# Masks of a chunked recurrence moved from GpSimd to VectorE, and an unread product left out

## The chip, the core and the metric

The kernel runs on one core of one Trainium2 chip. The core has a matrix engine (TensorE, in the profile PE, with its weight loads shown apart as PEld), a vector engine (VectorE, DVE), an engine for activation functions and copies (ScalarE, ACT), a general engine (GpSimd, POOL) and a queue that issues transfers (SyncE, SP). All work from SBUF, the memory on the chip; TensorE writes its results to PSUM, from which VectorE and ScalarE read them. The metric is the device time of one execution in microseconds (us), given as a median of several runs.

## The reference

The kernel computes one step of a decoder layer for 1024 prompt tokens and 32 sample tokens (8 sequences of 4). Cut to what matters here:

```
z = rmsnorm(x) @ w_in                        # columns for the recurrence and for pooling
h = x + [rwkv7(z_r) | pool(z_p)] @ w_out
h = h + peer(rmsnorm(h))                     # product keys: top-16 of 16384 experts, 8 heads
h = h + (p @ ple_w) * sigmoid(rmsnorm(h) @ ple_gate_w)
y = rmsnorm(h)

# inside rwkv7, per head, S is a 64 x 64 state:
s_kk = S @ (-kk_t)
S    = S * w_t + outer(s_kk, kk_t * a_t) + outer(v_t, k_t)
out  = S @ r_t
# then: out normalised per head (mean, variance), scaled, plus a bonus term, times a gate
```

## The kernel before

The work is a list of stages that overlap. **Stage A** (`phase_a`) projects all 1056 tokens, prepares the recurrence's inputs and writes them to the DRAM tile `fd`, seven groups of four blocks: a, r, b, k, v, g and o (the gate and bonus terms). It is followed by the pooling heads. **The recurrence** (`bchunk`, lines 446 to 619) runs over 16 chunks of 64 prompt tokens and one chunk for the 32 sample tokens. **Stage C** (`phase_c`) takes groups of 256 or 288 tokens through `w_out`, the norm and the query projection, and stores key scores in `sc_d`. **Top-k** (`top`, `select`) finds the experts of each token on VectorE and, for the first 672 token positions, builds one-hot products (lines 901 to 910) that give a dense gate table `g_d`. **The dense experts** (`ublock`, `vblock`, all through `emm`, line 1112) multiply these 672 tokens with all 16384 experts on TensorE, while the other 384 tokens gather their experts' rows (lines 1221 to 1238). `Tail` ends the layer.

The recurrence does not start with the others and end with them: `merge` (line 955) interleaves what the generators issue. Chunks 0 and 1 run beside pooling, the sample chunk with chunks 2 and 3, then chunk 4 beside the embedding products and the pooled half of `w_out`, and the rest beside stage C and top-k of three token groups. At most three chunks are in flight (`NSLOT`), begun at least six steps apart (`STAG`). Each has its own SBUF tiles, told apart by its slot; all take their PSUM tiles from one pool of four buffers. The final order on each engine's queue is not the order of the source: the program is built with a scheduler that plans every engine's queue ahead from estimated durations (line 1403). On the chip each queue then runs strictly in that order.

One chunk works on quads: the 8 heads are 4 pairs, and a pair's two 64 x 64 blocks lie on partitions 0 to 63 and 64 to 127, so a 64 x 64 product for all heads is 8 products, each of two instructions in the profile. All go through the helper `hmm`, so the profile names line 470 for each; GpSimd's steps go through `PTT` and have line 127. The steps of one chunk:

- **Products and their mask.** For each pair, b and k as weights against [a, r] together (line 491) give four 64 x 64 products: b by a, b by r, k by a, k by r. VectorE multiplies two pairs at a time out of PSUM with a causal mask into `lp` (line 492). The later steps read `lp[:, :, 1]`, `[2]` and `[3]` (lines 550, 569, 574); `lp[:, :, 0]`, b by a, is read by none.
- **Masked levels.** a against b (line 496) goes by ScalarE into SBUF as `lts` (line 498). The inverse of a triangular matrix is built in six levels (`NL`): level l needs `lts` times a constant mask `nmt[:, l]`, which GpSimd makes for each level (lines 501 and 512) in a tile `ltm` of two buffers. X starts as the first masked level plus the identity (GpSimd, line 508), Y as its transpose (TensorE, line 507, and ScalarE, line 509).
- **Levels 1 to 5.** TensorE multiplies `ltm` with Y, ScalarE copies the result to `zp`, TensorE multiplies it with X, and ScalarE copies X and Y back (lines 513 to 525).
- **State.** Transposes of b, k and v (lines 528 to 538), then w, u and the new state S (lines 548 to 597). Only this part needs the state of the chunk before.
- **Output.** Sums per head on VectorE (lines 602 to 604), the centred output `cen` (line 606, in the tile named `lts`), its square on ScalarE, the inverse root, then `cen` times the root on GpSimd (line 613), a transpose on TensorE, times g on VectorE (line 617) and plus o on GpSimd (line 618), then the store to `y_d`, which stage C reads.

Of the kernel before, what the change touches and what calls it, by code (L numbers as in the profile page):

```python
# [15 lines left out]
AF = mybir.ActivationFunctionType  # L16
ALU = mybir.AluOpType
# [46 lines left out]
def body(ctx, tc, io):  # L64
    nc = tc.nc
    mm = nc.tensor.matmul
    TT, STT, TS, ACT = (nc.vector.tensor_tensor, nc.vector.scalar_tensor_tensor, nc.vector.tensor_scalar,
                        nc.scalar.activation)
# [57 lines left out]
    def PTT(out, a, b, op):  # L126
        nc.gpsimd.tensor_tensor(out, a, b, op=op)  # L127

    def PS(tag):
        return pools[tag].tile([128, 512], F32, name="ps", tag="bc" if tag in ("b0", "b1") else tag)  # L130
# [9 lines left out]
    NL = 6  # L140
    HS = (slice(0, 64), slice(64, 128))
    nmt = rconst.tile([128, NL, 64], F32)
    mask64 = rconst.tile([128, 4, 64], F32)
    mask4 = rconst.tile([128, 4, 64], F32)
    ident2 = rconst.tile([128, 64], F32)
# [300 lines left out]
    def bchunk(c, sp=None):  # L446
        smpl = sp is not None
        slot = 1 if smpl else c % NSLOT
        pst = "b0"
# [3 lines left out]
        nlev = 2 if smpl else NL  # L453
        msk = mask4 if smpl else mask64

        def wt(name, n, bufs=1):
            return pb.tile([128, n], F32, name=name, tag=f"{name}{slot}", bufs=bufs)

        def q4(name, bufs=1):
            return v3(wt(name, 256, bufs), 64)  # L460

        def quad(ps):
            return v3(ps[:, :256], 64)

        def bc(ap):
            return ap[:, None, :].to_broadcast([128, 4, 64])

        def hmm(o, l, r, start, stop):
            for hs in HS:
                mm(o[hs], l[hs], r[hs], start=start, stop=stop)  # L470

        def pmm(o, l, r, start, stop):
            for p in range(4):
                hmm(o[:, p], l[:, p], r[:, p], start and (start != "one" or p == 0), stop and (stop != "one" or p == 3))
# [5 lines left out]
        f = sp[3] if smpl else pb.tile([128, 28, 64], F32, name="fdc", bufs=NSLOT + 1)  # L480
        nc.sync.dma_start(f[:, :, :tt], fd[:, :, ts])
        fa, fr, fb, fk, fv, fg, fo = (f[:, 4 * i:4 * i + 4] for i in range(7))
        lp = wt("lp", 1024).rearrange("m (q j t) -> m q j t", q=4, j=4)

        for pp in range(2):
            ps = PS(pst)
            pv = ps.rearrange("m (i q t) -> m i q t", i=2, q=4)
            for i in range(2):
                p = 2 * pp + i
                for k in range(2):  # L490
                    hmm(pv[:, i, 2 * k:2 * k + 2, :], f[:, 8 + 4 * k + p], f[:, p:8:4], True, True)
            TT(lp[:, 2 * pp:2 * pp + 2], pv, msk[:, None, :, :].to_broadcast([128, 2, 4, 64]), op=ALU.mult)
            yield

        ps = PS(pst)
        pmm(quad(ps), fa, fb, True, True)
        lts = q4("lts")
        ACT(lts, quad(ps), AF.Copy)
        yield
        x0 = q4("ltm", 2)  # L500
        PTT(x0, lts, bc(nmt[:, 0, :]), op=ALU.mult)
        yx = wt("yx", 512).rearrange("m (j q t) -> m j q t", j=2, q=4)
        Y, X = yx[:, 0], yx[:, 1]
        ps = PS(pst)
        hmm(ps[:, :256], id16[:, 0, :], id16.rearrange("m q t -> m (q t)"), True, False)
        for p in range(4):
            hmm(quad(ps)[:, p], x0[:, p], ident2, False, p == 3)
        PTT(X, x0, bc(ident2), op=ALU.add)
        ACT(Y, quad(ps), AF.Copy)
        for l in range(1, nlev):  # L510
            ltm = q4("ltm", 2)
            PTT(ltm, lts, bc(nmt[:, l, :]), op=ALU.mult)
            ps = PS(pst)
            hmm(ps[:, :256], id16[:, 0, :], id16.rearrange("m q t -> m (q t)"), True, False)
            pmm(quad(ps), ltm, Y, False, "one")
            zp = q4("zp")
            ACT(zp, quad(ps), AF.Copy)
            yield
            ps = PS(pst)
            n = 1 if l == nlev - 1 else 2  # L520
            pyx = ps.rearrange("m (j q t) -> m j q t", j=2, q=4)
            pmm(pyx[:, 0], X, zp, True, True)
            if n == 2:
                pmm(pyx[:, 1], zp, X, True, True)
            ACT(yx[:, :n], pyx[:, :n], AF.Copy)
            yield

        kbT = wt("kbT", 512).rearrange("m (j q t) -> m j q t", j=2, q=4)
        ps = PS(pst)
# [5 lines left out]
        ps = PS(pst)  # L535
        turn(quad(ps), fv)
        vt = q4("vt")
# [9 lines left out]
        s_in = S[-1]  # L547
        psw = PS(pst)
        pw = quad(psw)
        pmm(pw, lp[:, :, 2], vt, "one", False)  # L550
        if smpl:
            ssm, bmask, cmask = sp[:3]
            sp_ = ssm[0]
# [8 lines left out]
        u = q4("zp")  # L562
# [3 lines left out]
        def out():  # L566
            pso = PS(pst)
            po = quad(pso)
            pmm(po, lp[:, :, 3], vt, "one", False)
            if smpl:  # L570
                sample_s(fr, po, False)
            else:
                pmm(po, fr, s_in, False, False)
            pmm(po, lp[:, :, 1], u, False, "one")
            return po

        if smpl:
# [24 lines left out]
        s1 = wt("s1", 4)  # L602
        nc.vector.tensor_reduce(s1, po, axis=AX.X, op=ALU.add)
        TS(s1, s1, -1.0 / HD, None, op0=ALU.mult)
        cen = q4("lts")
        TT(cen, po, s1[:, :, None].to_broadcast([128, 4, 64]), op=ALU.add)
        sq = q4("wn")
        ACT(sq, cen, AF.Square)
# [1 line left out]
        nc.vector.tensor_reduce(s2, sq, axis=AX.X, op=ALU.add)  # L610
        inv_sqrt(s2, s2, 1.0 / HD, leps_t)
        yield
        PTT(cen, cen, s2[:, :, None].to_broadcast([128, 4, 64]), op=ALU.mult)
        ps = PS(pst)
        turn(quad(ps), cen)
        yo = v3(pb.tile([128, 256], F32, name="yo", tag=f"kbT{slot}"), 64)
        TT(yo, quad(ps), fg, op=ALU.mult)
        PTT(yo, yo, fo, op=ALU.add)
        nc.sync.dma_start(y_d[:, :, pos:pos + tt], yo[:, :, :tt])

    wraws = {}
# [799 lines left out]
```

## Time and profile before

| | us |
|---|---|
| median of 3 runs (3301.97 to 3302.18) | 3302.07 |
| the profiled execution | 3310.19 |
| its span, first to last instruction | 3308.5 |
| recurrence, first to last instruction of line 470 (about) | 285 to 1111 |
| dense experts without a pause, from (about) | 1345 |

The profile is one execution. "Busy" is the time in which an engine has an instruction under way; matmuls overlap, and a busy PE is not PE at its peak. "Idle before" is the time that an engine stood still in front of an instruction, with the one that released it. The chain is followed back from the last instruction, at each step to what released it. An instruction group reads: line, engine, operation, output and inputs, shape, count, then busy time and mean ns of one.

### The profile page before, as it was taken

Reading aid. Unit: us, or ns where it says so; the run is one execution under the profiler, and the core shown is the slowest. Engines: PE = TensorE matmul, PEld = TensorE weight load, DVE = VectorE, ACT = ScalarE, POOL = GpSimd, SP = SyncE. Lnnn points to the kernel's source line nnn. Section 1 sums busy time; section 2 is a strip of 40 time slices with the busy share of each in tenths; the row PEclk is TensorE's granted clock in tenths of the full one; section 3 lists DMA queues with packets and bytes.
Section 4 is the critical chain, followed back from the end, with each engine's and each line's share of the span. In section 5 each row is a group of like instructions: output and inputs, shape, how many; then the busy total and the mean of one; then the engine's idle time right before and its main releaser. Section 6 shows DMA issues by size and latency. Waiting matters only on the chain.

```text
span 3308.5 us, 66279 instructions
## 1 busy us (share of the span) xinstructions
PE 3115.4 (94%) x26777; PEld 2995.7 (91%) x26777; DVE 2561.4 (77%) x4989; ACT 1127.6 (34%) x1734; POOL 1509.4 (46%) x1223
## 2 busy tenths in 40 slices
PE   8998898987888798999999999999999999999997
PEld 7886787877877787999999999999999999999996
DVE  7775333469689688888888888888888888888966
ACT  6442423434554555332222122122222222212243
POOL 5212232222132041146666665666566666666534
PEclk9999999998998898999999999999999999999998
DMA  3325557866875977569999999999999999999834
GB/s 117 117 88 126 156 139 231 277 177 179 241 218 179 296 237 229 198 225 343 336 345 337 327 348 331 327 344 344 330 334 347 331 329 341 337 327 343 316 109 129
DMA packets 437332, 858.88 MB, mean 260 GB/s; under 512 B 108960, under 2 KB 232096, under 8 KB 432544
## 3 DMA queue, kind: packets, MB, share of 16 engines
q1 hardware_dynamic: 326432, 451.93, 42.1%
q0 software_dynamic: 110592, 402.70, 33.6%
q8 instruction: 210, 3.44, 0.4%
q14 instruction: 98, 0.80, 0.1%
HBM read 733.92 MB, written 120.60 MB: 258 GB/s over the span
## 4 chain that ended last, share of the span: by engine, by line
PE 77%; DVE 9%; DMA 8%; ACT 2%; issue 2%; POOL 1%; SPq 1%; ACTq 0%; DVEq 0%; POOLq 0%
PE pd L1112 58%; PE ps L470 5%; PE ps L219 4%; PE ps L653 2%; PE ps L655 2%; PE ps L654 2%; DMA whi<-wc_d 2%; PE ps L909 2%; PE ps L302 1%; DMA scq<-sc_d 1%; DMA sc_d<-scs 1%; DMA wlo<-wc_d 1%; DMA hT_d<-h 1%; PE ps L739 1%; DVE I L762 1%
## 5 line engine op out<-in xcount | busy, mean ns | idle before, releaser
L1221 POOL DMA_INDIRECT row<-u,idx x384 | 546.6, 1423 | 313.8 <-DVE row L1229 134.1
L1221 POOL DMA_INDIRECT row<-v,idx x384 | 536.5, 1397 | 310.8 <-DVE po L1238 142.0
L1088 ACT ACTIVATE ehi<-eraw 128x1024 fp32r<-128x1024 f32 x278 | 294.7, 1060 | 1115.0 <-PE pd L1112 1014.7
L1112 PE MATMUL pd<-XH,elo 128*128 128x336 f32 x2176 | 514.7, 318 | 4.7 <-DVE elo L1090 3.1
L1112 PE MATMUL pd<-XL,ehi 128*128 128x336 f32 x2176 | 515.4, 318 | 0.0
L1112 PE MATMUL pd<-XH,ehi 128*128 128x336 f32 x2176 | 513.4, 317 | 0.3 <-ACT ehi L1088 0.2
L1112 PE MATMUL pd<-wh,ehi 128*128 128x336 f32 (+1 forms) x2112 | 503.4, 317 | 6.5 <-DVE tg L1302 6.5
L1112 PE MATMUL pd<-wh,elo 128*128 128x336 f32 (+1 forms) x2112 | 503.7, 317 | 0.0
L1112 PE MATMUL pd<-wl,ehi 128*128 128x336 f32 (+1 forms) x2112 | 502.3, 317 | 0.0
L1238 DVE SCALAR_TENSOR_TENSOR po<-row,act,po 128x1024 f32<-128x1024 f32 x381 | 488.6, 1283 | 6.7
L1229 DVE SCALAR_TENSOR_TENSOR row<-row,xt 128x1024 f32<-128x1024 f32 x384 | 455.7, 1220 | 9.7 <-DMA row<-u,idx 6.3
L1112 PEld LDWEIGHTS pd<-XH,elo 128*128 128x128 f32 x2176 | 374.1, 189 | 5.7 <-DVE elo L1090 3.5
L1090 DVE TENSOR_TENSOR elo<-eraw,ehi 128x1024 fp32r<-128x1024 f32 x256 | 315.8, 1234 | 79.0 <-ACT ehi L1088 73.2
L1112 PEld LDWEIGHTS pd<-XH,ehi 128*128 128x128 f32 x2176 | 373.3, 189 | 1.1 <-ACT ehi L1088 0.7
L1112 PEld LDWEIGHTS pd<-XL,ehi 128*128 128x128 f32 x2176 | 372.0, 189 | 0.2
L1112 PEld LDWEIGHTS pd<-wh,ehi 128*128 128x128 f32 x2112 | 362.3, 188 | 7.2 <-issue 7.0
L1112 PEld LDWEIGHTS pd<-wl,ehi 128*128 128x128 f32 x2112 | 362.4, 188 | 0.0
L1112 PEld LDWEIGHTS pd<-wh,elo 128*128 128x128 f32 x2112 | 361.7, 188 | 0.2
L653 PE MATMUL ps<-hi,whi 128*128 128x256 f32 (+1 forms) x592 | 189.3, 322 | 48.7 <-DMA whi<-wc_d 21.1
L127 POOL TENSOR_TENSOR ltm<-lts,nmt 128x256 f32<-128x256 f32 x98 | 82.1, 846 | 311.8 <-PE ps L470 189.0
L1181 DVE TENSOR_TENSOR OT<-pd,OT 128x672 f32<-128x672 f32 x120 | 102.9, 858 | 142.8 <-PE pd L1112 142.1
L910 ACT ACTIVATE gst<-ps 128x512 f32<-128x512 f32 x168 | 169.5, 1110 | 67.1 <-PE ps L909 62.0
(426 smaller groups left out, 5256.2 us busy)
## 6 DMA issues: line engine op xcount, KB each, us to landing
eraw<-uT SPq DMA_DIRECT2D x128, 512.0 KB, 6.4
eraw<-vP SPq DMA_DIRECT2D x128, 512.0 KB, 6.4
g_d<-gst SPq DMA_DIRECT2D x21, 2048.0 KB, 9.8
gq<-g_d SPq DMA_DIRECT2D x32, 1344.0 KB, 9.6
whi<-wc_d SPq DMA_DIRECT2D x108, 256.0 KB, 4.9
wlo<-wc_d SPq DMA_DIRECT2D x108, 256.0 KB, 5.2
fdc<-fd SPq DMA_DIRECT2D x16, 896.0 KB, 7.6
wc_d<-whi SPq DMA_DIRECT2D x40, 256.0 KB, 4.6
```

What stands on the lines that cost most here:

```text
L127: nc.gpsimd.tensor_tensor(out, a, b, op=op)
L219: mm(ps[:, :XW], s[:, k, :], x[:, k, a:b], start=first, stop=last)
L470: mm(o[hs], l[hs], r[hs], start=start, stop=stop)
L653: mm(ps[:, :n], whi[:, kk, :], xhi[:, k, :n], start=k == 0, stop=False)
L910: ACT(st[:, :, t2 + q:t2 + q + 4].rearrange("p e t -> p t e"), v3(ps, 128), AF.Copy, scale=1.0 / GS)
L1088: ACT(hi, raw, AF.Copy)
L1090: sub(lo, raw, hi.bitcast(F32), op=ALU.subtract)
L1112: mm(ps[:, a, :n], w_[:, k, :], x_[:, s:s + n], start=first, stop=last)
L1181: TT(halves(OT[db]), ps[:, :, :NH], halves(OT[db]), op=ALU.add)
L1221: nc.gpsimd.indirect_dma_start(out=r[:m], out_offset=None, in_=io[tab], in_offset=bass.IndirectOffsetOnAxis(ap=idx[:m, hh, k:k + 1], axis=0))
L1229: STT(r[:m], r[:m], 1.0, xt[:m], op0=ALU.mult, op1=ALU.mult, accum_out=pre[:m, k:k + 1])
L1238: STT(po[:m], r[:m], act[:m, k:k + 1], po[:m], op0=ALU.mult, op1=ALU.add)
```

## The change

Four edits in `bchunk`, and nothing outside it:

- The a-by-b product comes first in a chunk and stays in PSUM. Two VectorE instructions multiply it, broadcast, with the masks of three levels each (one level each in the sample chunk, which has two) into an `ltm` tile of six levels. ScalarE's copy to `lts` and the six GpSimd masks go.
- X's first sum, the scaling of `cen` and the last addition of `yo` move from GpSimd to VectorE.
- b by a is no longer computed: b multiplies r alone, k multiplies [a, r], and `lp` has three parts instead of four, with the mask's last three quarters.
- `cen` lies in the tile named `zp`, since `lts` is gone. In SBUF, a slot has 1536 elements of `ltm` in place of 512, 768 of `lp` in place of 1024, and 256 fewer for `lts`.

```diff
-        lp = wt("lp", 1024).rearrange("m (q j t) -> m q j t", q=4, j=4)
+        lp = wt("lp", 768).rearrange("m (q j t) -> m q j t", q=4, j=3)
+        ps = PS(pst)
+        pmm(quad(ps), fa, fb, True, True)
+        ltm = wt("ltm", 256 * NL).rearrange("m (l q t) -> m l q t", l=NL, q=4)
+        for l0, l1 in ((0, nlev // 2), (nlev // 2, nlev)):
+            sh = [128, l1 - l0, 4, 64]
+            TT(ltm[:, l0:l1], quad(ps)[:, None].to_broadcast(sh), nmt[:, l0:l1, None, :].to_broadcast(sh), op=ALU.mult)
+        yield
         for pp in range(2):
             ps = PS(pst)
-            pv = ps.rearrange("m (i q t) -> m i q t", i=2, q=4)
+            pv = ps[:, :384].rearrange("m (i q t) -> m i q t", i=2, q=3)
             for i in range(2):
                 p = 2 * pp + i
-                for k in range(2):
-                    hmm(pv[:, i, 2 * k:2 * k + 2, :], f[:, 8 + 4 * k + p], f[:, p:8:4], True, True)
-            TT(lp[:, 2 * pp:2 * pp + 2], pv, msk[:, None, :, :].to_broadcast([128, 2, 4, 64]), op=ALU.mult)
-            yield
-
-        ps = PS(pst)
-        pmm(quad(ps), fa, fb, True, True)
-        lts = q4("lts")
-        ACT(lts, quad(ps), AF.Copy)
-        yield
-        x0 = q4("ltm", 2)
-        PTT(x0, lts, bc(nmt[:, 0, :]), op=ALU.mult)
+                hmm(pv[:, i, 0, :], f[:, 8 + p], f[:, 4 + p], True, True)
+                hmm(pv[:, i, 1:3, :], f[:, 12 + p], f[:, p:8:4], True, True)
+            TT(lp[:, 2 * pp:2 * pp + 2], pv, msk[:, None, 1:, :].to_broadcast([128, 2, 3, 64]), op=ALU.mult)
+            yield
+
+        x0 = ltm[:, 0]
...
-        PTT(X, x0, bc(ident2), op=ALU.add)
+        TT(X, x0, bc(ident2), op=ALU.add)
         ACT(Y, quad(ps), AF.Copy)
         for l in range(1, nlev):
-            ltm = q4("ltm", 2)
-            PTT(ltm, lts, bc(nmt[:, l, :]), op=ALU.mult)
             ps = PS(pst)
...
-            pmm(quad(ps), ltm, Y, False, "one")
+            pmm(quad(ps), ltm[:, l], Y, False, "one")
...
-        cen = q4("lts")
+        cen = q4("zp")
...
-        PTT(cen, cen, s2[:, :, None].to_broadcast([128, 4, 64]), op=ALU.mult)
+        TT(cen, cen, s2[:, :, None].to_broadcast([128, 4, 64]), op=ALU.mult)
...
-        PTT(yo, yo, fo, op=ALU.add)
+        TT(yo, yo, fo, op=ALU.add)
```

More of the change, by code (lines that the diff above doesn't have):

```diff
@@ L549, in bchunk @@
         pw = quad(psw)
-        pmm(pw, lp[:, :, 2], vt, "one", False)
+        pmm(pw, lp[:, :, 1], vt, "one", False)
         if smpl:
@@ L568, in out @@
             po = quad(pso)
-            pmm(po, lp[:, :, 3], vt, "one", False)
+            pmm(po, lp[:, :, 2], vt, "one", False)
             if smpl:
@@ L573, in out @@
                 pmm(po, fr, s_in, False, False)
-            pmm(po, lp[:, :, 1], u, False, "one")
+            pmm(po, lp[:, :, 0], u, False, "one")
             return po
```

## The prediction

> **What bounds the kernel now.** First the page: the span, the busy times, DVE's busy tenths over 40 slices of 82.7 us, and the chain that ended last, by engine and by line.
>
> ```profile
> span 3308.5 us, 66279 instructions
> PE 3115.4 (94%) x26777; PEld 2995.7 (91%) x26777; DVE 2561.4 (77%) x4989; ACT 1127.6 (34%) x1734; POOL 1509.4 (46%) x1223
> DVE  7775333469689688888888888888888888888966
> PE 77%; DVE 9%; DMA 8%; ACT 2%; issue 2%; POOL 1%; SPq 1%; ACTq 0%; DVEq 0%; POOLq 0%
> ```
>
> POOL is 46% busy but only 1% of the chain: most work that leaves POOL leaves no gap. Then the table of stretches: PE, PEld, DVE, ACT and POOL busy, with instruction counts, granted clock, DMA share and GB/s.
>
> ```profile
> 430.00:520.00 90.00, 90.00 (x1438) 80.25 (x1438) 30.56 (x60) 20.49 (x45) 23.69 (x30) 1.00 0.49 133
> 700.00:800.00 100.00, 73.44 (x1052) 65.39 (x1050) 95.83 (x511) 35.95 (x77) 33.18 (x51) 0.78 0.50 145
> 800.00:1110.00 310.00, 277.12 (x4030) 248.23 (x4030) 250.00 (x877) 163.45 (x285) 62.80 (x84) 0.92 0.75 220
> 1345.00:3308.00 1963.00, 1938.67 (x12549) 1934.18 (x12548) 1677.88 (x2381) 520.42 (x639) 1163.82 (x826) 0.99 0.85 307
> ```
>
> After 1345 us PE is busy 98.8% with the dense experts. The change does not touch that stage; it can only start it earlier or later. So everything is decided before 1345 us, and the recurrence runs only from about 285 to 1110 us. In there the limit changes: from 430 to 520 us PE has no gap at all; from 700 to 800 us DVE has none (95.83 of 100 us, top-k and one-hot work) and PE idles for it; from 800 to 1110 us both are filled, PE to 89% and DVE to 81%.
>
> **What leaves.** The groups of the recurrence between 285 and 1161 us (busy, mean ns, idle before):
>
> ```profile
> L127 POOL TENSOR_TENSOR ltm<-lts,nmt 128x256 f32<-128x256 f32 x98 | 82.1, 846 | 311.8 <-PE ps L470 189.0 <-ACT lts L498 122.3
> L127 POOL TENSOR_TENSOR yx<-ltm,ident 128x256 f32<-128x256 f32 x17 | 14.5, 851 | 0.0
> L127 POOL TENSOR_TENSOR lts<-lts,s 128x256 f32<-128x256 f32 x17 | 11.8, 695 | 107.9 <-DVE s L179 107.9
> L127 POOL TENSOR_TENSOR yo<-yo,fdc 128x256 f32<-128x256 f32 x16 | 13.2, 824 | 55.7 <-DVE yo L617 55.7
> L498 ACT ACTIVATE lts<-ps 128x256 f32<-128x256 f32 x17 | 6.5, 385 | 8.5 <-PE ps L470 8.1
> ```
>
> POOL loses 82.1 + 14.5 + 11.8 + 13.2 = 121.6 us and ACT 6.5 us. The large idle times before the POOL groups (311.8 us) are not a cost: POOL waits there for PE to give back a buffer or for ACT. What costs is PE waiting for somebody. The waits of PE from 285 to 1345 us (us in total, times, longest):
>
> ```profile
> PE ps L909 <- DVE ab L902: 19.6, 5, 8.9
> PE ps L470 <- POOL ltm L127: 5.2, 2, 4.4
> PE ps L470 <- ACT yx L509: 3.4, 2, 2.9
> PE ps L470 <- DVE lp L492: 3.0, 2, 2.4
> PE ps L470 <- POOL lo L127: 2.7, 1, 2.7
> ```
>
> *Masks on POOL.* PE waited 5.2 us for a masked level. I take all of it away: **-5.2 us** (bounds -5.2 and 0, if DVE is as late instead). *POOL's own queue.* POOL also splits activations for the projections (lo); one such split was late by 2.7 us, and the masks no longer stand ahead of it. Half: **-1.4 us** (0 to -2.7). *ACT's copy.* Y (L509) was late by 3.4 us. Its chain was copy 0.385 + POOL mask 0.846 and two hand-overs; it becomes one DVE mask of 0.96 us (below), 0.27 us and one hand-over shorter: **-1.0 us** (0 to -3.4).
>
> *Unread products.* The product of b with a (lp[:, :, 0]) is computed as one half of a 128-wide product with b as weights, and nobody reads it. PE's products in order of time (start, us, what) show the spacing:
>
> ```profile
> 568.10 0.63 PE L470 MATMUL ps<-yx,zp 64*64 64x64 f32 x16
> 568.57 1.04 PE L470 MATMUL ps<-fdc 64*64 64x128 f32 x16
> 569.44 0.63 PE L470 MATMUL ps<-wn,yx 64*64 64x64 f32 x16
> ...
> L470 PE MATMUL ps<-fdc 64*64 64x128 f32 x512 | 37.1, 278 | 0.0
> ```
>
> From one start to the next, sixteen 64-wide products take 0.47 us (29 ns each), sixteen 128-wide ones 0.87 us (54 ns). 512 over 16 chunks are 32 a chunk, of which 16 become 64 wide: 16 x 25 ns = 0.40 us a chunk, 6.4 us in all. PE is the limit in part of the recurrence only; half: **-3.2 us** (0 to -6.4).
>
> **What arrives on DVE.** Nearest rows: the lp mask itself, two 256-wide steps, and a 672-wide step that reads PSUM like the new masks (it lies in the dense stage).
>
> ```profile
> L492 DVE TENSOR_TENSOR lp<-ps,mask 128x512 f32<-128x512 f32 x34 | 23.3, 687 | 42.6 <-PE ps L470 42.6
> L606 DVE TENSOR_TENSOR lts<-ps,s 128x256 f32<-128x256 f32 x17 | 7.1, 421 | 0.6
> L596 DVE TENSOR_TENSOR S<-S,pcs 128x256 f32<-128x256 f32 x16 | 7.3, 458 | 0.2
> L1181 DVE TENSOR_TENSOR OT<-pd,OT 128x672 f32<-128x672 f32 x120 | 102.9, 858 | 142.8 <-PE pd L1112 142.1
> ```
>
> From 421 ns at 256 to 858 ns at 672 is 1.05 ns an element. A mask step of three levels has 768: 858 + 96 x 1.05 = 0.96 us, two of them 1.92 us. The sum X, the scaling of cen and the last addition of yo have two SBUF inputs, as L596 has: 0.46 us each. The two lp masks shrink from 512 to 384, by 0.13 us each. A chunk therefore adds 1.92 + 0.46 - 0.26 = 2.12 us at its start and 0.92 us at its end. Sixteen chunks are 48.6 us; the sample chunk (two levels, so two 256-wide masks) adds 2.0: DVE 2561 to 2612 us. Which of it is felt depends on when it falls due; the lp masks (two a chunk) and L606 (one) count starts and ends:
>
> ```profile
> 700.00:800.00 100.00, 2.01 (x3) 0.78 0.50 145
> 800.00:1110.00 310.00, 5.46 (x8) 0.92 0.75 220
> ...
> 700.00:800.00 100.00, 0.82 (x2) 0.78 0.50 145
> 800.00:1110.00 310.00, 2.51 (x6) 0.92 0.75 220
> ```
>
> From 700 to 800 us: 1.5 x 2.12 + 2 x 0.92 = 5.0 us, where DVE has no room: taken in full. From 800 to 1110 us: 4 x 2.12 + 6 x 0.92 = 14.0 us, where DVE shares the limit with PE and with loads of weights: a third, 4.7 us. The other 31.6 us fall before 700 us, where DVE is a third busy (30.56 of 90 us) and PE or loads cover it: nothing; without that cover it would be all 31.6. Together **+9.7 us** (bounds 0 and 19.0, or 50.6 with no cover anywhere).
>
> *The new wait.* The first mask now makes DVE, not ACT, wait for PE's a-by-b product; behind it stand the lp masks, the top-k steps and the one-hot products that PE's L909 reads. ACT idled 8.1 us for it in all. DVE already waits 42.6 us in front of the lp masks for the products issued next to it, so that wait moves ahead rather than comes on top: nothing (0 to +8.1). X follows on DVE, cen follows its own reciprocal, yo its own product: no wait. No DMA is added; y's store is released 0.36 us earlier a chunk. The PSUM buffer of the product is held 1.9 us instead of 0.4; four such buffers serve three chunks, and I put no price on it beyond rival 1.
>
> *Stretched DVE steps.* Two rows over all their instances (min/median/max):
>
> ```profile
> L902 DVE TENSOR_TENSOR ab<-ab,e x84: 662/684/2887, 765.4 to 1313.8; 128x1024 f16<-128x1024 f16 x84
> L127 POOL TENSOR_TENSOR ltm<-lts,nmt x98: 717/731/2577, 288.1 to 1044.5; 128x256 f32<-128x256 f32 x98
> L902 DVE TENSOR_TENSOR ab<-ab,e 128x1024 f16<-128x1024 f16 x62 | 45.4, 740 | 0.5
> 285.00:1161.00 876.00, 209.77 (x272) 0.91 0.68 202
> ```
>
> Steps of equal shape reach four times their median. For L902 the excess is 62 x (740 - 684) ns = 3.5 us; POOL gives up 121.6 of its 209.8 busy us there, so 0.58 x 3.5: **-2.0 us** (0 to -3.5). [...]
>
> **Sum.** -5.2 - 1.4 - 1.0 - 3.2 + 9.7 - 2.0 = -3.1 us. The profiled execution took 3310.19 us (span 3308.5 and 1.7 around it), 8.1 over the median of 3302.07; nothing in the difference touches the terms, so -3.1 goes on both: about 3307.1 profiled and **3299.0 us** as median. About 0.2% (6.6 us) is what a measurement of this kernel can tell from no change.
>
> **Rivals.**
> 1. *DVE becomes the bound from 700 us on: slower.* All 19.0 us that fall between 700 and 1110 us are felt, because each chunk's masks stand in DVE's queue ahead of the one-hot products for which PE already waits 19.6 us. Of the gains (12.8) half remains, since PE then waits for DVE in place of POOL: 19.0 - 6.4 = +12.6, 3314.7 us. It decides if DVE's share from 800 to 1110 us goes from 81% to over 90%. For it: 95.83 of 100 us. Against: DVE's gaps of 60 us there.
> 2. *The order tightens: clearly faster.* The engines' orders are laid out ahead by a planner. For the first chunk the mask is done by 288.8 us, but PE takes its first reader at 290.75, after a run of projection products:
>
> ```profile
> 288.06 1.42 POOL L127 TENSOR_TENSOR ltm<-lts,nmt 128x256 f32<-128x256 f32 x2 [7.64 <-ACT lts L498]
> 290.50 0.32 PE L655 MATMUL ps<-xhi,wlo 128*128 128x352 f32 x1
> ```
>
>    If masks from one engine let each of 16 chunks start 1 us earlier in places where PE now idles, that is 16 us more: -19.1, 3283.0 us. Against: PE worked in those 2 us.
> 3. *Nothing is felt:* removed and added steps lie beside projections and loads of weights. 3302 us.
>
> **How the numbers follow.** Forecast 0.45 (its own range 3290 to 3309: part of it, 0.16, lies under 3295.5, 0.03 over 3308.7), rival 1 0.22, rival 2 0.25, rival 3 0.08. Faster: 0.16 + 0.25 = 0.41; slower 0.03 + 0.22 = 0.25; same 0.26 + 0.08 = 0.34. The range reaches to both outer rivals, 3281 to 3316 us; it covers the bounds of the terms except 50.6 with no cover.
>
> **What would show it.** POOL near 1388 us busy, ACT 1121, DVE 2612; mask steps of 0.96 us, lp masks of 0.55; no wait of PE for ltm on POOL; 700 to 800 us still full on DVE; the dense stage's steady run as long as before, starting within a few us of 1345. The forecast is wrong if PE's waits for DVE steps grow by more than 10 us (rival 1), or if PE's idle time before 1110 us shrinks by more than 15 us (rival 2).

## The result and the profile after

| | before | after |
|---|---|---|
| median of 6 runs, us (lowest to highest) | 3302.12 (3300.49 to 3310.99) | 3274.63 (3272.34 to 3278.57) |
| the profiled execution, us | 3310.19 | 3273.07 |
| its span, us | 3308.5 | 3271.4 |

The ratio of after to before is 0.9913, with a 95% interval of 0.9903 to 0.9923: 0.87% or some 27 us faster. The forecast was 3299.0 us, its range 3281 to 3316, so the time fell below the range. The two profiled executions lie 37 us apart, 10 more than the medians, since the profiled one of before was a long one. Among the runs of the experiments a few executions (one each of e2 and e6, two of the kernel before) took 23 to 99% longer than the others; the ratios leave them out, and as the profiled execution of e2 was one of them, nothing is read from its profile.

First the page of after: the span, the busy times and the chain by engine.

```profile
span 3271.4 us, 66102 instructions
PE 3090.2 (94%) x26777; PEld 2972.0 (91%) x26777; DVE 2595.2 (79%) x5074; ACT 1117.0 (34%) x1714; POOL 1390.7 (43%) x1074
PE 76%; DVE 12%; DMA 8%; ACT 2%; issue 1%; POOL 1%; SPq 1%; ACTq 0%; DVEq 0%; POOLq 0%
```

POOL fell by 118.7 us, ACT by 10.6, and DVE grew by 33.8. PE has as many instructions as before, but is 25.2 us less busy and has 11.9 us fewer gaps (3271.4 - 3090.2 = 181.2, against 193.1). The new steps, from the groups of after between 285 and 1161 us (busy, mean ns, idle before):

```profile
L901 DVE TENSOR_TENSOR ab<-ab,e 128x1024 f16<-128x1024 f16 x66 | 48.8, 744 | 0.1
L490 DVE TENSOR_TENSOR ltm<-ps,nmt 128x768 f32<-128x768 f32 x32 | 29.0, 948 | 16.1 <-PE ps L470 16.1
L499 DVE TENSOR_TENSOR lp<-ps,mask 128x384 f32<-128x384 f32 x34 | 18.7, 551 | 18.0 <-PE ps L470 17.9
L509 DVE TENSOR_TENSOR yx<-ltm,ident 128x256 f32<-128x256 f32 x17 | 7.9, 462 | 0.0
L612 DVE TENSOR_TENSOR zp<-zp,s 128x256 f32<-128x256 f32 x17 | 7.3, 432 | 0.3
L617 DVE TENSOR_TENSOR yo<-yo,fdc 128x256 f32<-128x256 f32 x16 | 7.0, 439 | 0.2
```

The steps cost what the prediction gave them. So the missing time is not in the price of a step. To find it, mark the stages by stage C's loads of the recurrence's output (`y<-y_d`, one per token group) and by the first load of the dense gates (`gq<-g_d`). Rows of these tiles, before and then after: durations min/median/max, first and last start.

```profile
L619 SPq DMA_DIRECT2D y_d<-yo x17: 518/550/6012, 362.5 to 1116.8; - x17
L683 SPq DMA_DIRECT2D y<-y_d x4: 572/574/1206, 518.0 to 1159.8; - x4
L1166 SPq DMA_DIRECT2D gq<-g_d x32: 319/327/563, 1331.8 to 3010.6; - x32
```

```profile
L618 SPq DMA_DIRECT2D y_d<-yo x17: 524/554/7332, 336.6 to 1095.6; - x17
L682 SPq DMA_DIRECT2D y<-y_d x4: 565/577/577, 519.8 to 1114.8; - x4
L1165 SPq DMA_DIRECT2D gq<-g_d x32: 319/327/422, 1286.1 to 2972.3; - x32
```

The recurrence stores its first output 26 us earlier (336.6 against 362.5 us), but this does not last: in the traces the four loads of y start at 518, 692, 938 and 1160 us before, and at 520, 691, 907 and 1115 after; the first dense gates are loaded at 1332 and 1286. At the second load the gain is 2 us; 29 come on top between the second and the third, 14 between the third and the fourth, and next to nothing from there to the first dense load. Of these 46 us the end keeps 37. So three stages decide, from the second load (690 us) to the first dense load. Now the table of stretches over them, as PE, PEld, DVE, ACT and POOL busy with instruction counts, then clock, DMA share and GB/s; the first row is an earlier stretch, the last a fixed one that serves to compare many kernels below. Before:

```profile
430.00:520.00 90.00, 90.00 (x1438) 80.25 (x1438) 30.56 (x60) 20.49 (x45) 23.69 (x30) 1.00 0.49 133
690.00:938.00 248.00, 208.18 (x3105) 186.84 (x3107) 199.78 (x774) 122.23 (x223) 56.38 (x81) 0.89 0.70 202
938.00:1160.00 222.00, 181.96 (x2405) 162.25 (x2401) 178.88 (x683) 104.71 (x180) 43.69 (x59) 0.87 0.75 231
1160.00:1332.00 172.00, 149.53 (x1200) 143.03 (x1201) 149.24 (x589) 92.90 (x130) 53.00 (x47) 0.91 0.77 236
690.00:1345.00 655.00, 551.80 (x6790) 503.76 (x6791) 534.42 (x2051) 323.58 (x537) 158.81 (x187) 0.89 0.74 224
```

After, with the same stages at their new places:

```profile
430.00:520.00 90.00, 90.00 (x1338) 81.42 (x1336) 32.74 (x63) 19.82 (x43) 0.14 (x1) 1.00 0.44 129
690.00:907.00 217.00, 190.38 (x2972) 172.09 (x2967) 196.53 (x788) 112.47 (x208) 24.40 (x44) 0.94 0.75 219
907.00:1115.00 208.00, 174.04 (x2468) 155.68 (x2464) 180.75 (x732) 102.38 (x180) 26.13 (x35) 0.90 0.79 243
1115.00:1286.00 171.00, 145.30 (x1202) 136.25 (x1201) 150.70 (x530) 94.67 (x132) 54.84 (x45) 0.92 0.80 250
690.00:1345.00 655.00, 564.66 (x6999) 517.54 (x6995) 576.16 (x2249) 331.66 (x549) 117.88 (x136) 0.92 0.77 235
```

In the first of the three stages DVE does about the same work in both kernels (199.78 and 196.53 us), but in 217 us instead of 248: its gaps fall from 48.2 to 20.5 us. PE's gaps fall from 39.8 to 26.6 us, and PE itself is busy 17.8 us less, at a granted clock of 0.94 instead of 0.89 and with 2972 products in place of 3105. Over all three stages, 642 us before and 596 after, DVE's work is the same (527.9 and 528.0 us), so its gaps fall by the whole 46 us, from 114.1 to 68.0. PE's gaps fall by 16 us, from 102.3 to 86.3, and PE is busy 30 us less; the last section shows how its clock has a part in this. Over the fixed stretch from 690 to 1345 us DVE's gaps go from 655 - 534.4 = 120.6 to 655 - 576.2 = 78.8 us; this understates the gain a little, since the stretch reaches further into the dense experts after the change. What DVE waited for in the three stages, from 690 to 1332 us before:

```profile
L901 DVE TENSOR_TENSOR ab<-iota,e 128x2048 f16<-128x2048 f16 x84 | 103.5, 1238 | 50.1 <-PE ps L909 49.8
L761 DVE MAX8 V<-scq 128x8 f32<-128x128 f32 x96 | 21.4, 277 | 32.1 <-DMA scq<-sc_d 32.1
L492 DVE TENSOR_TENSOR lp<-ps,mask 128x512 f32<-128x512 f32 x12 | 8.2, 680 | 9.6 <-PE ps L470 9.6
L603 DVE TENSOR_REDUCE s<-ps 128x4 f32<-128x256 f32 x8 | 3.3, 414 | 9.2 <-PE ps L470 9.2
```

And from 690 to 1286 us after:

```profile
L900 DVE TENSOR_TENSOR ab<-iota,e 128x2048 f16<-128x2048 f16 x84 | 106.1, 1267 | 21.1 <-PE ps L908 18.2 <-ACT e L886 2.8
L760 DVE MAX8 V<-scq 128x8 f32<-128x128 f32 x92 | 21.3, 279 | 18.8 <-DMA scq<-sc_d 18.8
L490 DVE TENSOR_TENSOR ltm<-ps,nmt 128x768 f32<-128x768 f32 x12 | 10.9, 947 | 7.4 <-PE ps L470 7.4
L499 DVE TENSOR_TENSOR lp<-ps,mask 128x384 f32<-128x384 f32 x12 | 6.6, 548 | 1.3 <-PE ps L470 1.3
L602 DVE TENSOR_REDUCE s<-ps 128x4 f32<-128x256 f32 x8 | 3.3, 413 | 1.0 <-PE ps L470 1.0
```

None of these four waits of before is directly a wait for GpSimd. DVE waited for products and for key scores, on steps that the change does not touch or only makes smaller, and in the new order of its queue and PE's it waited less: 32 us less for PE at the one-hot products, 13 us less for scores, 8 us less for the reduction of the output. The waits for scores have in part only moved into the dense stage: over the whole span they are 43.1 us before and 50.0 after.

### The profile page after: what moved, and what is told of

Its sections match the earlier page's. It is cut to its first block, busy times and chain, and to the rows that moved or that the text cites. A ratio compares the mean times of both kernels' runs of the same rounds, so it can differ in the third digit from the quotient of the medians.

```text
span 3271.4 us, 66102 instructions
## 1 busy us (share of the span) xinstructions
PE 3090.2 (94%) x26777; PEld 2972.0 (91%) x26777; DVE 2595.2 (79%) x5074; ACT 1117.0 (34%) x1714; POOL 1390.7 (43%) x1074
## 4 chain that ended last, share of the span: by engine, by line
PE 76%; DVE 12%; DMA 8%; ACT 2%; issue 1%; POOL 1%; SPq 1%; ACTq 0%; DVEq 0%; POOLq 0%
PE pd L1111 58%; PE ps L470 5%; PE ps L219 4%; PE ps L652 2%; PE ps L654 2%; PE ps L653 2%; DVE ab L900 1%; DMA scq<-sc_d 1%; PE ps L302 1%; DMA sc_d<-scs 1%; PE ps L908 1%; DMA wlo<-wc_d 1%; DVE ab L901 1%; DMA whi<-wc_d 1%; PE ps L1018 1%
## 5 line engine op out<-in xcount | busy, mean ns | idle before, releaser
L1089 DVE TENSOR_TENSOR elo<-eraw,ehi 128x1024 fp32r<-128x1024 f32 x256 | 317.0, 1238 | 80.0 <-ACT ehi L1087 77.4
L1111 PEld LDWEIGHTS pd<-wh,ehi 128*128 128x128 f32 x2112 | 362.5, 188 | 7.1 <-issue 6.9
L654 PE MATMUL ps<-hi,wlo 128*128 128x256 f32 (+1 forms) x592 | 181.1, 307 | 7.6 <-DMA wlo<-wc_d 7.1
```

The costliest lines, as they stand in the source:

```text
L654: l = mm(ps[:, :n], wlo[:, kk, :], xhi[:, k, :n], start=False, stop=k == K - 1)
L1089: sub(lo, raw, hi.bitcast(F32), op=ALU.subtract)
L1111: mm(ps[:, a, :n], w_[:, k, :], x_[:, s:s + n], start=first, stop=last)
```

## The experiments

The edits are named here by letters: **M**, the six masks as two VectorE steps; **S**, the three other steps (X, `cen`, `yo`) on VectorE; **O**, a by b first in a chunk; **P**, the product left out. The changed kernel is M+S+O+P. In the recorded expectations, theory A is that M pays, B that any edit makes the planner lay another order and the time scatters with it, C that P pays, D that O pays, E that it pays to take a chunk wholly off GpSimd. All medians stand beside runs of the kernel before on the same chip, and the ratio is to these.

| kernel | parts | median us | ratio to before (95%) |
|---|---|---|---|
| e1_masks | M O | 3265.48 | 0.9879 (0.9863 to 0.9895) |
| f1_masks_steps | M S O | 3269.45 | 0.9895 (0.9875 to 0.9915) |
| c3_after_tiny | M S O P, tiny copies | 3278.13 | 0.9904 (0.9888 to 0.9921) |
| u1_after_old_order | M S P | 3276.99 | 0.9907 (0.9890 to 0.9923) |
| the changed kernel | M S O P | 3274.63 | 0.9913 (0.9903 to 0.9923) |
| f2_masks_products_tiny | M O P, tiny copies | 3278.94 | 0.9918 (0.9893 to 0.9942) |
| c2_masks_tiny | M O, tiny copies | 3280.25 | 0.9934 (0.9911 to 0.9956) |
| f4_after_dummy_gpsimd | M S O P, GpSimd kept at work | 3285.52 | 0.9937 (0.9916 to 0.9958) |
| f3_steps_reorder | S O | 3286.39 | 0.9941 (0.9921 to 0.9961) |
| e5_reorder | O | 3287.07 | 0.9948 (0.9935 to 0.9961) |
| e3_products | P | 3289.97 | 0.9957 (0.9943 to 0.9971) |
| d1_lp_last | M S O P, lp later | 3296.67 | 0.9965 (0.9950 to 0.9980) |
| c1_before_tiny | tiny copies | 3300.60 | 0.9983 (0.9973 to 0.9994) |
| e4_masks_products | M O P | 3300.22 | 0.9987 (0.9978 to 0.9996) |
| e2_steps | S | 3302.27 | 0.9992 (0.9982 to 1.0002) |
| u2_products_reorder | O P | 3303.19 | 0.9993 (0.9983 to 1.0002) |
| e6_masks_late | M | 3307.98 | 1.0006 (0.9994 to 1.0019) |
| g1_after_masks_x5 | M S O P, masks five times | 3308.49 | 1.0017 (1.0007 to 1.0027) |
| g2_before_lp_x7 | lp masks seven times | 3317.80 | 1.0043 (1.0027 to 1.0060) |

**One part at a time, and two together.** The masks with the a-by-b product first, all else as before:

```diff
+        ps = PS(pst)
+        pmm(quad(ps), fa, fb, True, True)
+        ltm = wt("ltm", 256 * NL).rearrange("m (l q t) -> m l q t", l=NL, q=4)
+        for l0, l1 in ((0, nlev // 2), (nlev // 2, nlev)):
...
-        lts = q4("lts")
-        ACT(lts, quad(ps), AF.Copy)
...
-        PTT(x0, lts, bc(nmt[:, 0, :]), op=ALU.mult)
+        x0 = ltm[:, 0]
```

> Masks alone: the a-by-b product first, its six masks by two VectorE steps out of PSUM; X, cen and yo stay on GpSimd, b by a is computed and masked as before. Theory A (the masks on GpSimd held the chunks back; without them the planner lays the queues closer from 690 us on): most of the 27 us, 3275 to 3285 us, and VectorE's gaps between 690 and 1160 us shrink from 91 us to under 65. Theory B (no one part: any edit makes the planner lay another order, worth plus or minus 10 us): 3290 to 3312 us. Theory C (the gain is TensorE's, from the product left out): 3302 us or more.

The three other steps alone:

```diff
-        PTT(X, x0, bc(ident2), op=ALU.add)
+        TT(X, x0, bc(ident2), op=ALU.add)
...
-        PTT(cen, cen, s2[:, :, None].to_broadcast([128, 4, 64]), op=ALU.mult)
+        TT(cen, cen, s2[:, :, None].to_broadcast([128, 4, 64]), op=ALU.mult)
...
-        PTT(yo, yo, fo, op=ALU.add)
+        TT(yo, yo, fo, op=ALU.add)
```

> X, cen and yo alone on VectorE; masks on GpSimd from a copy in SBUF, all products as before. Theory A: small, 3296 to 3304 us, since these steps have no later step of the recurrence's state behind them, except X. Theory B: 3290 to 3312 us, either sign. If the end of a chunk (cen, yo, store of y) is what stage C waits for, 3285 to 3295 us.

The unread product left out, alone:

```diff
-                for k in range(2):
-                    hmm(pv[:, i, 2 * k:2 * k + 2, :], f[:, 8 + 4 * k + p], f[:, p:8:4], True, True)
+                hmm(pv[:, i, 0, :], f[:, 8 + p], f[:, 4 + p], True, True)
+                hmm(pv[:, i, 1:3, :], f[:, 12 + p], f[:, p:8:4], True, True)
```

> The product b by a left out alone (it was read by nobody), lp masks 384 wide. Theory A: 6.4 us less for TensorE and 4.4 us less for VectorE, of which half is felt at most: 3296 to 3302 us. Theory C: most of the 27 us, under 3285 us. Theory B: 3290 to 3312 us.

The changed kernel with the three steps of e2 turned back to GpSimd (the minus and plus lines above exchanged):

> The changed kernel with X, cen and yo back on GpSimd. Theory A: within 5 us of the changed kernel, 3270 to 3285 us. If the three steps matter as much as the masks, 3285 to 3295 us. Theory B: anywhere from 3265 to 3300 us.

The parts do not add. e1 gave -1.21% and e3 -0.43%; together, in e4, they gave -0.13%. And e2 gave nothing, but e4 and the changed kernel differ only in these steps and are 0.74% apart. The stretch from 690 to 1345 us, first e1 and then e4:

```profile
690.00:1345.00 655.00, 573.70 (x7044) 526.52 (x7045) 576.83 (x2247) 336.49 (x553) 130.51 (x158) 0.93 0.77 235
```

```profile
690.00:1345.00 655.00, 553.20 (x6850) 505.31 (x6849) 550.12 (x2096) 320.85 (x532) 132.85 (x150) 0.89 0.75 227
```

GpSimd has the same load in both (130.5 and 132.9 us), yet e1 has gaps of 78.2 us on DVE and e4 of 104.9. So the load that GpSimd loses does not settle the time; it goes with how closely the work of DVE and PE is packed.

**Is it the order, or chance?** The place of the a-by-b product alone; the masks at the old place; and two controls that hold the same work as before and as e1, plus 34 copies of four elements on DVE.

```diff
+        ps = PS(pst)
+        pmm(quad(ps), fa, fb, True, True)
+        lts = q4("lts")
+        ACT(lts, quad(ps), AF.Copy)
+        yield
...
-        ps = PS(pst)
-        pmm(quad(ps), fa, fb, True, True)
-        lts = q4("lts")
-        ACT(lts, quad(ps), AF.Copy)
-        yield
```

> The kernel before with only the order of a chunk's first steps turned: a by b and ScalarE's copy come first, the lp products after; masks on GpSimd, no work changed. Theory A (the engine of the masks counts): 3295 to 3305 us. Theory D (the order counts: a by b first lets the levels start earlier): 3262 to 3285 us. Theory B (any edit makes another plan): anywhere from 3265 to 3310 us.

e6 is e1 with the masks where a by b stood before, behind the lp masks:

> e1_masks with the old order: the lp products first, then a by b and its two VectorE mask steps. Theory A: as e1_masks, 3260 to 3272 us. Theory D: back at 3295 to 3305 us. Theory B: anywhere from 3265 to 3310 us.

```diff
-            TT(lp[:, 2 * pp:2 * pp + 2], pv, msk[:, None, :, :].to_broadcast([128, 2, 4, 64]), op=ALU.mult)
+            TT(lp[:, 2 * pp:2 * pp + 2], pv, msk[:, None, :, :].to_broadcast([128, 2, 4, 64]), op=ALU.mult); nc.vector.tensor_copy(wt("tiny", 4), lp[:, 2 * pp, 0, 0:4])
```

> A control: the kernel before with one VectorE copy of 4 elements behind each lp mask (34 steps of about 0.1 us, nobody reads them), so that the work is the same to 4 us and the planner lays another order. Theories A and D: 3300 to 3308 us. Theory B: off by 8 us or more, to either side.

> The same control on e1_masks. Theories A and D: 3263 to 3271 us. Theory B: off by 8 us or more, most likely slower, since e1_masks is the best of five.

The order alone gave -0.52%, the masks in the old order nothing. But the copy moved e1 from 0.9879 to 0.9934, 0.55% or 18 us, while the 34 copies take a median of 0.17 us each (c1's expectation had put 0.1), some 6 us together. A single kernel's ratio thus says little about the part it was made for: much of it is the plan that this kernel happened to get. The plan is what the copy changes: if the traces of before and c1 are compared by operation, source line and tile, some 3000 of PE's 26777 products stand in another order, the first at 705 us and nearly all of them ahead of the dense stage. That the queues run in the planned order shows in the trace of before: the 1687 steps of ACT and the 389 two-input steps of POOL stand in it as the built program has them, and so do those of DVE and PE, counted as runs of one line and tile (2787 and 3035 runs).

**Several plans for each mixture.** The changed kernel in the old order; order and product without the masks; the changed kernel with the tiny copies; and the changed kernel with the lp products moved further back, just ahead of w (more of what theory D holds to pay).

> The changed kernel with one part undone: the lp products first again, a by b and its masks behind them. Theory D (the new order of a chunk's first steps brings the gain, by some 18 us in the mean over plans): 3290 to 3305 us. Theory A (masks off GpSimd bring it): 3268 to 3280 us. Theory B alone (plans scatter by some 12 us about one mean for both orders): no telling, 3275 to 3300 us.

> e3_products with the new order: a by b first, the masks still on GpSimd. Theory D: faster than e3_products by 5 to 25 us, 3265 to 3285 us. Theory A: as e3_products, 3286 to 3294 us.

> The control of 34 small VectorE copies on the changed kernel: how far another plan of the same work lies from it. Theory D with scatter: 3265 to 3295 us. Without scatter: 3275 to 3279 us.

> The changed kernel with the lp products moved further back, to just ahead of their first reader (w). Theory D (what counts is that the levels begin early and that products nobody waits for do not stand in front): as the changed kernel or faster, 3255 to 3280 us. If only the masks' place at the head of VectorE's queue counted: the same. If lp's products are late for w there: slower, 3285 us or more.

With masks and steps both moved, the kernel with the old order is as fast (u1 0.9907), and the tiny copies change nothing (0.9904). d1 lost more than half of the gain, so pushing the lp products back did not pay in this plan. Then the two mixtures still missing, e4 with the tiny copies, and a kernel that gives GpSimd its six mask steps a chunk back, into a tile `dum` that nobody reads:

> The changed kernel with the unread product b by a computed and masked again; masks and X, cen, yo on VectorE. Theory E (a chunk with nothing on GpSimd is what pays: GpSimd runs its queue in order, and the chunk's steps there held up, and were held up by, the steps of top-k and stage C on the same queue): 3268 to 3285 us, like the three kernels with everything moved (ratios 0.9913, 0.9907, 0.9904). Theory B (plans scatter about one mean): 3265 to 3305 us.

> X, cen and yo on VectorE and a by b first, masks on GpSimd. Theory E: 3290 to 3305 us, the masks still being on GpSimd. If the three steps with the new order make it: 3268 to 3285 us.

> The control of 34 small copies on e4_masks_products (masks moved, X, cen and yo on GpSimd, product left out), which was at 0.9987. Theory E: 3290 to 3305 us, since three steps are still on GpSimd; the two fast kernels of this kind (0.9879 and 0.9934) are then the scatter. If masks alone make it: 3265 to 3285 us.

```diff
+        PTT(v3(pb.tile([128, 256], F32, name="dum", bufs=1), 64), x0, bc(nmt[:, 0, :]), op=ALU.mult)
...
+            PTT(v3(pb.tile([128, 256], F32, name="dum", bufs=1), 64), ltm[:, l], bc(nmt[:, l, :]), op=ALU.mult)
```

> The changed kernel plus the six mask steps of each chunk on GpSimd again, from VectorE's ltm into a tile that nobody reads: GpSimd has its work and its waits back, and TensorE waits for none of it. Theory E (GpSimd's queue is what costs): 3290 to 3305 us. If it is only that TensorE, or the plan of TensorE, no longer depends on GpSimd's results: 3270 to 3285 us.

The same stretch of f1, then of f4:

```profile
690.00:1345.00 655.00, 575.23 (x7066) 525.09 (x7065) 581.86 (x2241) 340.88 (x558) 114.34 (x136) 0.93 0.77 236
```

```profile
690.00:1345.00 655.00, 555.74 (x6970) 505.32 (x6970) 564.00 (x2127) 331.78 (x548) 147.02 (x164) 0.92 0.76 231
```

f4 puts GpSimd at 147 us, near the 158.81 of before, and keeps 0.63% of the 0.87%. The 0.24% between them are within what a new plan does. So GpSimd's load is at most a part of it, and f4 leaves open whether that part is there.

Held against the recorded expectations, no theory fits all runs. A (masks) holds in u1, but e4 (3300 us) and e6 (3308 us) have the masks moved and are not fast. C (the product) fails: e3 alone reaches 3290 us, and f1 is fast without it. D (the order) fails in u1, 3277 us where it gave 3290 or more, and in u2, 3303 us where it gave 3285 or less. E (nothing left on GpSimd) holds in f1, but f2 has three steps on GpSimd and is at 3279 us where E gave 3290 or more; f3 and f4, both at 3286 us, lie between the ranges of E and of its rival. B (scatter) is seen where the same parts with and without the copies lie apart, e1 and c2 by 0.55% and e4 and f2 by 0.69%; but c1 moved by 5.5 us only, less than the 8 that B named, and c3 by 0.09%.

The 16 kernels that are mixtures of M, S, O and P, with or without the tiny copies (before among them, without d1, f4, g1 and g2), can be fitted by one amount per part: M -0.32%, S -0.28%, O -0.30%, P +0.03%, each with a standard error of 0.17 to 0.19, and 0.33% (11 us) of scatter left for the single kernel. By groups: neither M nor S, five kernels, mean 0.9976; S without M, two, 0.9967; M without S, five, 0.9945, scattered from 0.9879 to 1.0006; M and S, four, 0.9905, all within 0.9895 to 0.9913. Leaving out the product alone cannot be told from nothing.

**What DVE's work costs.** Two kernels that repeat DVE steps without changing a value: on the changed kernel each mask step five times, on the kernel before each lp mask seven times.

```diff
-        for l0, l1 in ((0, nlev // 2), (nlev // 2, nlev)):
+        for l0, l1 in ((0, nlev // 2), (nlev // 2, nlev)) * 5:
```

> The changed kernel with each mask step issued five times (the same values written again): 8 more VectorE steps of 0.96 us in a chunk, 126 us in all, some 45 us of them from 690 us on. If VectorE's added work is felt there in full, as the slow rival of the forecast had it: 3310 to 3330 us. If a third is felt (the forecast's price): 3280 to 3300 us. If gaps take it up: 3268 to 3282 us.

```diff
-            TT(lp[:, 2 * pp:2 * pp + 2], pv, msk[:, None, :, :].to_broadcast([128, 2, 4, 64]), op=ALU.mult)
+            for _ in range(7): TT(lp[:, 2 * pp:2 * pp + 2], pv, msk[:, None, :, :].to_broadcast([128, 2, 4, 64]), op=ALU.mult)
```

> The kernel before with each lp mask issued seven times: 12 more VectorE steps of 0.69 us in a chunk, 140 us in all, some 45 us of them from 690 us on. Felt in full: 3340 to 3360 us. A third: 3310 to 3330 us. Taken up by the gaps (120 of 655 us from 690 to 1345 us): 3290 to 3310 us.

The repeated groups from 690 to 1160 us and the stretch to 1345 us, g1 first, then g2:

```profile
L490 DVE TENSOR_TENSOR ltm<-ps,nmt 128x768 f32<-128x768 f32 x60 | 55.1, 942 | 7.4 <-PE ps L470 7.4
690.00:1345.00 655.00, 552.94 (x6790) 503.17 (x6787) 587.64 (x2161) 323.16 (x533) 111.60 (x128) 0.90 0.73 222
```

```profile
L492 DVE TENSOR_TENSOR lp<-ps,mask 128x512 f32<-128x512 f32 x84 | 55.8, 672 | 9.1 <-PE ps L470 9.0
690.00:1345.00 655.00, 549.66 (x6817) 500.45 (x6814) 571.38 (x2118) 321.88 (x537) 157.27 (x187) 0.89 0.73 221
```

In g1 these steps take 55.1 - 10.9 = 44.2 us more after 690 us, and the time is 1.04% above that of the changed kernel (1.0017 less 0.9913), 34 us: 0.77 of the added work, a high bound, as there is more of it before 690 us too. In g2 they take 55.8 - 8.2 = 47.6 us more and the time grows by 0.43%, 14 us: 0.30. With a plan's scatter of 11 us either way both shares are rough. But the direction fits the gaps: where DVE had 120.6 us of them (before), they soaked up most of the added work and shrank to 83.6; where it had 78.8 (after), less fits in (67.4 are left in g1). Of the recorded ranges, g2 lies in the one for a third, and g1, at 3308 us, between the one for a third and the one for the full amount.

## Why the prediction was wrong

**The bound of the stage.** Right in kind: almost nothing before 690 us counted (PE has no gap from 430 to 520 us in either kernel, and the 26 us of the first store are gone at the first load of y, at 518 and 520 us), and the stages of DVE and PE from 690 us decide. But DVE's 250 of 310 us between 800 and 1110 us were read as a limit that added work lengthens. They were also 60 us of gaps, and between 690 and 1345 us 120.6, which a better packing can win.

**The removed waits** (-5.2, -1.4, -1.0). No wait of PE for a masked level is left. But of the 11.3 us that these three terms are taken from, only 0.8 lay in the stages that decide, from 690 to 1345 us of before (us in total, times, longest):

```profile
PE ps L470 <- POOL ltm L127: 0.8, 1, 0.8
PE ps L909 <- DVE ab L903: 3.7, 5, 1.3
```

The row of 2.7 us (POOL lo) was also misread as a late split for a projection. The product that waited is one of the recurrence, and it reads yx and ltm, not lo; ScalarE had just written yx:

```profile
523.68 0.57 ACT L525 ACTIVATE yx<-ps 128x512 f32<-128x512 f32 x1
524.40 1.12 PE L470 MATMUL ps<-yx,ltm 64*64 64x64 f32 x16 [2.74 <-POOL lo L127]
```

So, as far as these rows show, the term of -1.4 had no wait for a split behind it. PE's waits for one-hot steps, the ground of rival 1, were 19.6 us (the prediction quotes the row) and the 3.7 above. They became these from 690 to 1345 us of after:

```profile
PE ps L908 <- DVE ab L901: 18.9, 12, 3.7
PE ps L908 <- DVE ab L902: 10.9, 11, 2.3
```

That is 29.8 in place of 23.3 us: 6.5 more, under the 10 us that would have spoken for rival 1; DVE's share from 800 to 1110 us went to 271.05 of 310 us (87%, below its 90%). The rival's mechanism may be at work, but it did not become the bound; and since the whole order changed, the 6.5 us are no proof of it.

**The unread product** (-3.2). The fit gives +0.03% with a standard error of 0.18%, 6 us either way; the term is neither borne out nor refuted.

**The added work on DVE** (+9.7). The sizes held: 948 ns for a mask step (0.96 us predicted), 551 for lp (0.55), 462, 432 and 439 for the steps with two SBUF inputs (460), POOL 1390.7 (1388), ACT 1117 (1121). DVE grew by 33.8 us to 2595 and not by the 50.6 of the sum (2612), though the steps that the change adds and removes come to some 49; the rest of DVE's steps take some 15 us less of its time, and no run shows why. The share taken, 9.7 of 19.0 us from 700 us on, is 0.51 and lies between the 0.30 and 0.77 that g2 and g1 measured, roughly, so nothing points to this term as the error.

**The wait moved ahead** (0). Right: DVE's 42.6 us before the lp masks became 16.1 before the mask steps and 18.0 before the lp masks.

**Stretched steps** (-2.0). The term takes it that POOL's work makes DVE's steps longer, and that the excess shrinks with that work. No run shows what lengthens them, nor that proportion. What the trace of before shows is that the two fall together: the 128 `ab<-ab,e` steps (lines 902 and 903) that overlap no POOL step took 662 to 694 ns, the 40 that overlap one had means of 1183 (line 902) and 861 ns (line 903) and reached 2887. After, there is no clear sign of a gain: in the row that the prediction used, the one-hot step `ab<-ab,e` has a mean of 744 ns (740 before). From 690 to 1345 us, over all 84 steps of that line, the mean falls from 784 to 729 ns, but the step ahead of it, `ab<-iota,e`, rises from 1238 to 1267. The trace of before also shows that the share of 0.58 was too much: all ten `ab<-ab,e` steps that take over 1.1 us (the median is 0.68) overlap a POOL step with two inputs in SBUF, but only four of them overlap a step that leaves POOL, and the three longest (2.8 to 2.9 us) overlap POOL's splits `elo`, which stay.

**The step that failed** is the sum's premise, which it does not state, that the queues keep their order and only the priced waits and steps change. Waits that could be removed came to 11.3 us even in full, and all but 0.8 of them lay ahead of 690 us. The planner lays all queues anew for any edit, and from 690 us on the gaps of PE and DVE, which the sum left at their value, are where the time lay: between marks of the same work DVE's fell by 46 us (32 of them waits for PE at the one-hot products) and PE's by 16, and PE ran less of its work at half clock (last section); the three stages became 46 us shorter, the span 37. The dense stage, which the prediction had start within a few us of 1345, loads its first gates 46 us earlier. Rival 2 (the order tightens, 0.25) was of the right kind and was left out of the sum, but its size (16 us) came from 2 us in front of the first chunk's first product, in a place where in the end nothing was gained. The sign that the prediction named for it, PE's idle time before 1110 us shrinking by more than 15 us, did not show, because it counts over a fixed stretch. The recurrence's whole stretch, before and then after:

```profile
285.00:1110.00 825.00, 719.65 (x11267) 646.79 (x11267) 488.01 (x1712) 345.31 (x684) 206.15 (x270) 0.92 0.66 195
```

```profile
285.00:1110.00 825.00, 717.90 (x11435) 646.63 (x11432) 537.35 (x1870) 352.12 (x686) 91.83 (x122) 0.94 0.70 208
```

PE's gaps there are 105.4 us before and 107.1 after, but the fixed stretch holds more work after (11435 matmuls in place of 11267). Between the loads of y, where about the same work is compared, they shrank by 13.2 and 6.1 us.

Over the 17 profiled kernels without g1, g2 and e2 the span goes with the gaps of DVE and of PE from 690 to 1345 us (correlation 0.93 for each), and much less with GpSimd's busy time there (0.42). That is a correlation: gaps are the other side of a longer stage, whichever engine starts them. It is shown that moving masks and steps together gave 0.87 to 1.05% in four plans (and 0.35% in d1, whose lp products stand elsewhere), that the unread product need not go for it (f1), and that most of it stays when GpSimd gets its load back (f4). Since e1 and f2 gained 1.21 and 0.82% with the three steps still on GpSimd, it is not shown that masks and steps must move together. Why plans without those hand-overs to GpSimd pack more closely stays open; that each hand-over is a point at which the planner's estimates and the chip can part is a guess that no run tests. What M, S or O is worth alone stays open within about 0.2%. The fastest of the kernels is e1, at 3265.48 us, faster than both; since its twin with the tiny copies is at 3280.25, its lead over the changed kernel is best put down to its plan.

## What to carry to other kernels

Where a planner lays the queues, compare an edit with neutral twins (the same work and a few tiny copies) before believing a difference of half a per cent, and make the parts in several mixtures. Price a change not only by the waits that it removes: add up the gaps of each engine that is nearly full in the deciding stage (here, from 690 to 1345 us of before, DVE with 82% and PE with 84%), between marks of the same work and not between fixed times, since these gaps are what a better order can win (here 46 us of DVE's) and what can soak up added work (in g2 DVE's gaps shrank from 120.6 to 83.6 us). Ask of each removed wait whether it lies in that stage: here the gains ahead of a stretch in which PE was full already were gone behind it.

## What the chip showed that was not expected

A gap on PE can cost more than its length. The table of stretches of before, in steps of 8 us from 760 to 800 us:

```profile
760.00:768.00 8.00, 1.86 (x22) 1.48 (x22) 8.00 (x23) 0.44 (x2) 0.00 (x0) 0.50 0.00 0
768.00:776.00 8.00, 7.66 (x53) 6.50 (x53) 8.00 (x20) 3.12 (x8) 7.95 (x9) 0.70 0.21 77
776.00:784.00 8.00, 4.21 (x52) 3.35 (x52) 8.00 (x49) 6.80 (x11) 1.58 (x3) 0.94 1.01 327
784.00:792.00 8.00, 8.00 (x110) 7.32 (x109) 7.79 (x32) 3.05 (x5) 1.10 (x1) 0.63 0.66 208
792.00:800.00 8.00, 8.00 (x126) 7.40 (x125) 6.94 (x24) 6.05 (x12) 0.74 (x1) 1.00 1.10 266
```

In the first row PE stands still for most of the time and the granted clock is 0.50. In the second PE is busy again, but its mean clock is still 0.70. The third has gaps of 3.8 us at a mean clock of 0.94, and the drop comes behind them: 0.63 in the fourth row, where PE has no gap, and 1.00 only in the last. So in these rows the clock follows PE's gaps with a delay, down and up. The clock records of the trace hold two values only, 0.5 and 1. They have it at half from 759.18 to 772.83 us; PE stood still from 759.08 to 766.14, and the full clock is back 6.7 us after that. And they have it at half from 783.07 to 789.90: the gaps of PE ahead of that lie between 777.64 and 783.83, so the drop comes 5.4 us after the first of them began and the full clock 6.1 us after the last one ended. The 0.63 of the fourth row thus stands for 5.9 of 8 us at half clock. At half clock the products come further apart, from one start to the next (medians in the trace of before): 107 ns in place of 57 for those of line 909, 280 in place of 153 for the 336-wide ones of line 1112. The mean clocks of the two profiled executions:

```profile
core 0: 3308.5 us, clock 0.968
```

```profile
core 0: 3271.4 us, clock 0.973
```

Span times (1 - clock) is 106 us before and 88 after, but this includes half clock while PE stood still. If the clock records are laid over PE's busy time in the traces, PE worked at half clock for 160 us before and 116 after, and half of that, 80 and 58 us, is about the most that the slow clock can have cost, an estimate from the 1.8 to 1.9 times of these spacings. The difference of 22 us would be most of the 25.2 us by which PE is less busy. In the three stages that decide it worked at half clock for 115 us before and 72 after: up to 21 of the 30 us by which it is less busy there. This was missing from the sum: closing a gap of PE can also win back time in the slow products behind it, by this estimate up to 21 us in the three stages.
